# Decoder layer on one core: residual loads moved into the second phase of the down projection, output stores on two queues, three activation splits moved to the end of its first phase

## The chip, the cores and the metric

The kernel runs on one core of one Trainium2 chip. The metric is the device time of one execution in microseconds (us), the median of several runs. A core has five engines that run side by side, each with its own instruction queue worked in order: TensorE (PE, matrix products into the PSUM banks), VectorE (DVE), ScalarE (ACT), GpSimd (POOL) and SyncE (SP), which here only issues transfers (DMAs). ACT can issue DMAs too. Engines wait for each other through semaphores.

## The reference

One decoder layer on 512 positions of 1024 channels in float32: a mixer (a gated matrix memory beside a convolution group), then a convolutional feed-forward block. The change lies in the last lines of the feed-forward block:

```python
def rms_norm(x, g):
    xf = x.astype(jnp.float32)
    y = xf * lax.rsqrt(jnp.mean(xf * xf, axis=-1, keepdims=True) + EPS)
    return (y * g.astype(jnp.float32)).astype(x.dtype)
...
        u = rms_norm(x, ffn_pre_g[l]) * (1.0 + sc2) + sh2
        up = causal_dwconv(u @ ffn_up[l], ffn_conv_w[l], ffn_conv_b[l])
        a, gt = jnp.split(up, 2, axis=-1)
        f = (jax.nn.silu(gt) * a) @ ffn_down[l]
        x = x + g2 * rms_norm(f, ffn_post_g[l])
```

Here `x` on the right is the residual (the mixer's output with its own residual added), `f` the down projection of 2816 channels back to 1024, and `g2` a gate per channel.

## The kernel before

**Number format.** Every large product is made of three matmuls on split operands: a float32 tile is split into a high half (rounded by ACT, `S.activation(hi, src, AF.Copy)`) and a low half (the rest, a subtraction on DVE). `split` (line 925) does it for the down projection; `mm3` (line 186) issues the three matmuls. A matmul of this kind has 128 rows of weights or activations as its stationary operand and 512 columns.

**The down projection** multiplies by a seven-product scheme of Strassen's kind over a 2 x 2 blocking (two halves of the tokens, two halves of the channels on either side). It runs over NM = 11 blocks m of 256 hidden channels, in two phases, since the products and their banks do not fit at once.

- Phase one (the loop at line 1056): `forms1(m)` makes the weight combinations of block m on DVE and splits four of them; `prod1` adds products p1, p5, p7 and p6, two token tiles each (q = 0, 1), 24 matmuls a block. For m = 9 and 10 the products are ordered one by one (line 1067), so that each result can be drained while the next is made. The combination that phase two needs again goes to memory (`t2_d`).
- Phase two (line 1102): `forms_g2(m)` splits the activations of block m, which had been stored to memory by `forms` during the up projection and are read back by `load_g2(m)` into one of five buffers (`kept`): two 256-wide forms side by side (profile names g2h, g2l) and a third (s). `forms2(m)` makes and splits three weight tiles (b, b, t in the profile), loaded by `load2(m)`. `prod2` adds products p2, p3, p4: 18 matmuls a block. For m = 9 and 10 the matmuls stand in the tail, token tile by token tile.
- The tail (line 1113) runs over the four token tiles tt: the last 6 or 12 matmuls, the sum of products (DVE, line 1127), its squares summed on ACT (`sq_sum`, line 610), the factor 1/rms (DVE line 615, POOL line 617), the gate (line 1130), and at line 1134 the factor times the row plus the residual `xr`. The residual stands in memory as `x1_d`, two halves of 512 channels a token tile, written long before. It is loaded on SP at line 1121 into tiles of a pool of four (`cvtile`), and the output rows are stored on SP at line 1135.

**Who sets the order.** On SP and PE the instructions run in the order of the source. On ACT, DVE and POOL a scheduler orders them when the kernel is built, by its own estimate of when operands are there. A tile from a pool waits until the tile that had its buffer before has been read by all its readers: `slot` has 44 buffers, which in phase one hold all split activations (`pairs`, 4 for each of 11 blocks); the weight halves have 20 (`wpool`), and the raw weights four places in all. On SP, the reload `load_g2(m + 5)` needs the buffer of activation m, so it waits for `forms_g2(m)`.

Of the kernel before, what the change touches and what calls it, by code (L numbers as in the profile page):

```python
# [19 lines left out]
T = 512  # L20
KT = D // P
NT = T // P
# [30 lines left out]
def decoder_layer(ctx, tc, w_glu0, x, c, adaT, vecs, w_glu, w_qko, w_v0, w_v, w_out, w_up, w_down, out):  # L53
    nc = tc.nc
# [29 lines left out]
    def slot(name, dt=F32):  # L84
        return slots.tile([P, T], dt, tag="t", name=name)
# [100 lines left out]
    def mm3(ps, a, b, start, stop):  # L186

        PE.matmul(ps, a[0], b[0], start=start, stop=False)  # L188
        PE.matmul(ps, a[0], b[1], start=False, stop=False)  # L189
        PE.matmul(ps, a[1], b[0], start=False, stop=stop)  # L190
# [79 lines left out]
    xr = [slot(f"xr{j}") for j in range(KT)]  # L270
# [10 lines left out]
    def u_tiles(name):  # L281
        hi = upool.tile([P, KT, T], F32R, tag="uh", name=f"{name}h")
        lo = upool.tile([P, KT, T], F32R, tag="ul", name=f"{name}l")
        return hi, lo, [(hi[:, j, :], lo[:, j, :]) for j in range(KT)]

    _, _, u = u_tiles("u")
# [316 lines left out]
    x1_d = [[dram.tile([P, T], F32, tag=f"x1d{tt}_{hf}", name=f"x1d{tt}_{hf}") for hf in range(2)] for tt in range(NT)]  # L603

    def cvtile(name):
        return cvs.tile([P, T], F32, tag="cvs", name=name)

    def sq_sum(src, col, name):
        junk = small.tile([P, T], BF16, tag="junk", bufs=1, name=f"{name}junk")
        S.activation(junk, src, AF.Square, accum_out=col)  # L610

    def token_factor(sq, name):

        t = small.tile([P, 1], F32, tag="tt", name=f"{name}t")
        V.tensor_scalar(out=t, in0=sq[:, :1], scalar1=sq[:, 1:2], scalar2=D * EPS, op0=ALU.add, op1=ALU.add)  # L615
        r = small.tile([P, 1], F32, tag="tr", name=f"{name}r")
        G.tensor_tensor(out=r, in0=t, in1=mhalf[:, :1], op=ALU.pow)  # L617
        return r

    def tok(tt):  # L620
        return slice(tt * P, (tt + 1) * P)
# [298 lines left out]
    NM = NF // 2  # L920
# [4 lines left out]
    def split(src, hi, lo):  # L925
        S.activation(hi, src, AF.Copy)
        V.tensor_tensor(out=lo, in0=src, in1=hi.bitcast(F32), op=ALU.subtract)
# [51 lines left out]
    M2 = NM - 2  # L979
# [11 lines left out]
    def parts(r, names):  # L991
        out = {}
        for name, b in names:
            hi, lo = wpool.tile([P, T], F32R, tag="w", name=f"{name}h"), wpool.tile([P, T], F32R, tag="w", name=f"{name}l")
            split(r[:, b * T : (b + 1) * T], hi, lo)
            out[name[:2]] = (hi, lo)
        return out

    def quarter(r, b):
        return r[:, b * T : (b + 1) * T]  # L1000
# [3 lines left out]
    def load1(m):  # L1004
        loaded[m] = r = wd_raw(m, 1)
        nc.sync.dma_start(r[:, T:], w_down[m][:, T:])

    def forms1(m):

        r = loaded.pop(m)  # L1010
        t3, b11, b12, b22 = (quarter(r, b) for b in range(4))
        V.tensor_tensor(out=t3, in0=b22, in1=b12, op=ALU.subtract)
        V.tensor_tensor(out=b12, in0=b12, in1=b11, op=ALU.subtract)
        V.tensor_tensor(out=b22, in0=b22, in1=b12, op=ALU.subtract)
        w = parts(r, [(f"b1_{m}", 1), (f"t1_{m}", 2), (f"t3_{m}", 0), (f"t2_{m}", 3)])
        nc.sync.dma_start(t2_d[m], b22)
        return w

    def load2(m):
        loaded[m] = r = wd_raw(m + NM, 2)  # L1020
        nc.sync.dma_start(r[:, :T], w_down[m][:, :T])
        nc.sync.dma_start(r[:, T : 2 * T], w_down[m][:, 3 * T :])
        nc.sync.dma_start(r[:, 2 * T : 3 * T], t2_d[m])

    def forms2(m):

        r = loaded.pop(m)
        V.tensor_tensor(out=quarter(r, 2), in0=quarter(r, 0), in1=quarter(r, 2), op=ALU.subtract)
        return parts(r, [(f"b2_{m}", 0), (f"b4_{m}", 1), (f"t4_{m}", 2)])

    def load_g2(m):
        nc.sync.dma_start(kept[:, m % 5, :], g2_d[m])

    def forms_g2(m):
        r = kept[:, m % 5, :]
        h, l, s = slot(f"g2h{m}", F32R), slot(f"g2l{m}", F32R), slot(f"s4{m}", F32R)
        split(r[:, :T], h, l)
        split(r[:, T:], s[:, :HT], s[:, HT:])
        return [(h[:, :HT], l[:, :HT]), (h[:, HT:], l[:, HT:]), (s[:, :HT], s[:, HT:])]

    def part(form, q):
        return tuple(z[:, q * P : (q + 1) * P] for z in form)
# [4 lines left out]
    def prod1(m, which):  # L1047
        (a11, s3), (s1, s2) = (halves_of(z) for z in pairs[m])
        ps, form, w = {"p1": (p1, a11, "b1"), "p5": (p5, s1, "t1"), "p7": (p7, s3, "t3"), "p6": (p6, s2, "t2")}[which]
        for q in range(2):  # L1050
            mm3(ps[q], part(form, q), w1[m][w], m == 0, m == NM - 1)

    w1, w2, g2 = {}, {}, {}
    for m in range(3):
        load1(m)
    for m in range(NM):
        w1[m] = forms1(m)
        if m + 3 < NM:
            load1(m + 3)
        else:  # L1060
            load2(m + 3 - NM)
        if m < 5:
            load_g2(m)
        if m < M1:
            for which in ("p1", "p5", "p7", "p6"):
                prod1(m, which)
# [26 lines left out]
    def prod2(m, which, q):  # L1093
        a12, a22, s4 = g2[m]
        ps, form, w = {"p2": (p2, a12, "b2"), "p3": (p3, s4, "b4"), "p4": (p4, a22, "t4")}[which]
        mm3(ps[q], part(form, q), w2[m][w], m == 0, m == NM - 1)
# [2 lines left out]
        sq_sum(sp5[q], fsq[:, 2 * (2 + q) + 1 : 2 * (2 + q) + 2], f"c22_{q}")  # L1099
    for q in range(2):  # L1100
        V.tensor_tensor(out=sp5[q], in0=sp5[q], in1=g2r[1], op=ALU.mult)
    for m in range(NM):
        g2[m] = forms_g2(m)
        w2[m] = forms2(m)
        if m + 3 < NM:
            load2(m + 3)
        if m + 5 < NM:
            load_g2(m + 5)
        if m < M2:
            for which in ("p2", "p3", "p4"):  # L1110
                for q in range(2):
                    prod2(m, which, q)
    for tt in range(NT):
        q = tt % 2
        for which in ("p2", "p3") if tt < 2 else ("p4",):
            for m in range(M2, NM):
                prod2(m, which, q)
        res, xr = [], []
        for hf in range(2):
            xr.append(cvtile(f"xr{tt}_{hf}"))  # L1120
            nc.sync.dma_start(xr[hf], x1_d[tt][hf])
        for hf, pair in enumerate(((p2[q], sp1[q]), (p3[q], su[q])) if tt < 2 else ((p4[q], s3[q]), None)):
            if pair is None:
                res.append(sp5[q])
                continue
            ps, z = pair
            V.tensor_tensor(out=z, in0=ps, in1=z, op=ALU.add)
            sq_sum(z, fsq[:, 2 * tt + hf : 2 * tt + hf + 1], f"dn{tt}_{hf}")
            m = slot(f"fo{tt}_{hf}")
            V.tensor_tensor(out=m, in0=z, in1=g2r[hf], op=ALU.mult)  # L1130
            res.append(m)
        r = token_factor(fsq[:, 2 * tt : 2 * tt + 2], f"ro{tt}")
        for hf in range(2):
            V.scalar_tensor_tensor(out=res[hf], in0=res[hf], scalar=r, in1=xr[hf], op0=ALU.mult, op1=ALU.add)
            nc.sync.dma_start(out[tok(tt), hf * T : (hf + 1) * T], res[hf])


def _layout(i):
# [65 lines left out]
```

## Time and profile before

| | |
|---|---|
| median of 3 runs | 794.95 us (794.9 to 799.16) |
| the profiled execution | 795.99 us, its span 794.3 us |
| busy: PE | 763.7 us (96%) |
| busy: DVE | 591.8 us (75%) |
| busy: ACT | 408.3 us (51%) |
| busy: POOL | 384.0 us (48%) |
| granted PE clock, mean | 0.99 |
| DMA | 124.28 MB, 156 GB/s from and to memory |

The span runs from the first to the last instruction; the execution's own time holds 1.7 us more around it. All times in the views are us from the start of the span. A row of a timeline has start, length, engine, source line, operation, output and inputs by the program's names (buffer numbers and digits left out, so the quarters t1, t2 and t3 of a block all appear as t), then the shape; in square brackets stands the idle time of the engine before it and what ended that. DVE and ACT overlap the end of one instruction with the start of the next, so the cost of one is the distance between starts. Phase one runs from 669 to 729 us, phase two from there to 777, and the span's last 17 us have no matmul.

### The profile page before, as it was taken

The page shows a single profiled execution, that of the slowest core. Times are in us where ns is not written, and L with a number is a line of the kernel's source. Part 1 is how long each engine was busy: PE and PEld are TensorE (multiplying, and loading weights), DVE is VectorE, ACT ScalarE, POOL GpSimd, SP SyncE. Part 2 cuts the span into 40 slices and gives each one's busy share as a digit, 9 for nine tenths or more (in the row PEclk, how much of TensorE's full clock was granted, in tenths as well). Part 3 has the DMA queues.
Part 4 walks back from the last instruction along what each step waited for, and adds up shares of the span by engine and source line. Part 5 has one row for each costly group of instructions (what it writes and reads, how often), then busy time and mean ns, then how long its engine had stood idle before and what let it go on. Part 6 is the DMA issues. An engine that isn't in the chain of part 4 may idle for free.

```text
span 794.3 us, 10575 instructions
## 1 busy us (share of the span) xinstructions
PE 763.7 (96%) x3683; PEld 636.6 (80%) x3683; DVE 591.8 (75%) x938; ACT 408.3 (51%) x766; POOL 384.0 (48%) x313
## 2 busy tenths in 40 slices
PE   7999999899999999999999999999999999998991
PEld 4778898678888888888889988888888888886880
DVE  6659999999997434546868796665665567997964
ACT  6576428658664455471344454444444434556641
POOL 3789749769788434342851475444444420000001
PEclk9999999999999999999999999999999999999996
DMA  8972312313127331425954654333333222973925
GB/s 290 332 294 106 108 54 106 132 33 110 66 72 230 129 133 54 160 106 206 350 186 151 210 191 152 104 101 121 127 126 116 88 101 97 356 254 98 349 72 185
DMA packets 35977, 124.28 MB, mean 156 GB/s; under 512 B 4146, under 2 KB 5586, under 8 KB 29908
## 3 DMA queue, kind: packets, MB, share of 16 engines
q1 hardware_dynamic: 24660, 96.20, 34.8%
q10 hardware_dynamic: 11264, 27.41, 9.7%
q8 instruction: 29, 0.48, 0.2%
q14 instruction: 24, 0.20, 0.1%
HBM read 112.17 MB, written 11.42 MB: 156 GB/s over the span
## 4 chain that ended last, share of the span: by engine, by line
PE 72%; DVE 15%; DMA 6%; ACT 3%; issue 2%; POOL 1%; SPq 0%; DVEq 0%; POOLq 0%; ACTq 0%
PE up L190 10%; PE up L189 10%; PE up L188 10%; DVE cv L661 5%; PE p L190 3%; PE p L188 3%; PE p L189 3%; PE glu L189 3%; PE glu L190 3%; PE glu L188 3%; PE qko L189 2%; PE qko L188 2%; PE qko L190 2%; PE mixa L190 2%; PE mixa L188 2%; PE mixa L189 2%
## 5 line engine op out<-in xcount | busy, mean ns | idle before, releaser
L661 DVE SCALAR_TENSOR_TENSOR cv<-gt,cvw,cv 128x506 f32<-128x506 f32 (+24 forms) x200 | 134.3, 729 | 0.4
L617 POOL TENSOR_TENSOR ro0r<-ro0t,mhalf 128x1 f32<-128x1 f32 x1 | 0.9, 922 | 128.9 <-DVE ro0t L615 128.9
L171 POOL TENSOR_TENSOR wup_1024l<-wup,wup_1024h 128x512 fp32r<-128x512 f32 x20 | 27.7, 1383 | 31.7 <-ACT wup_1024h L170 31.7
L171 POOL TENSOR_TENSOR wup_0l<-wup,wup_0h 128x512 fp32r<-128x512 f32 x20 | 27.8, 1388 | 29.5 <-ACT wup_0h L170 29.5
L657 POOL TENSOR_TENSOR cs<-cs,cs 128x510 f32<-128x510 f32 (+3 forms) x32 | 41.8, 1306 | 0.2
L171 POOL TENSOR_TENSOR wup_1536l<-wup,wup_1536h 128x512 fp32r<-128x512 f32 x20 | 28.4, 1421 | 27.2 <-ACT wup_1536h L170 27.2
L189 PE MATMUL up<-u2l,wup_0h 128*128 128x512 f32 (+1 forms) x100 | 36.5, 365 | 0.2 <-DVE u2l L830 0.2
L188 PE MATMUL up<-u2h,wup_0h 128*128 128x512 f32 (+1 forms) x100 | 36.5, 365 | 0.0
L188 PE MATMUL up<-u2h,wup_1024h 128*128 128x512 f32 (+1 forms) x100 | 36.5, 365 | 0.0
L190 PE MATMUL up<-u2h,wup_512l 128*128 128x512 f32 (+1 forms) x100 | 36.4, 364 | 0.0
L189 PE MATMUL up<-u2l,wup_1536h 128*128 128x512 f32 (+1 forms) x100 | 36.4, 364 | 0.0
L190 PE MATMUL up<-u2h,wup_0l 128*128 128x512 f32 (+1 forms) x100 | 36.4, 364 | 0.0
L190 PE MATMUL up<-u2h,wup_1536l 128*128 128x512 f32 (+1 forms) x100 | 36.4, 364 | 0.0
L188 PE MATMUL up<-u2h,wup_1536h 128*128 128x512 f32 (+1 forms) x100 | 36.4, 364 | 0.0
L188 PE MATMUL up<-u2h,wup_512h 128*128 128x512 f32 (+1 forms) x100 | 36.4, 364 | 0.0
L189 PE MATMUL up<-u2l,wup_512h 128*128 128x512 f32 (+1 forms) x100 | 36.4, 364 | 0.0
L190 PE MATMUL up<-u2h,wup_1024l 128*128 128x512 f32 (+1 forms) x100 | 36.4, 364 | 0.0
L189 PE MATMUL up<-u2l,wup_1024h 128*128 128x512 f32 (+1 forms) x100 | 36.4, 364 | 0.0
L155 DVE SCALAR_TENSOR_TENSOR junk<-ada,cb 128x1024 bf16<-128x1024 f32 x20 | 30.5, 1525 | 7.5 <-DMA ada<-in_adaT 7.2
L171 POOL TENSOR_TENSOR wup_512l<-wup,wup_512h 128x512 fp32r<-128x512 f32 x20 | 27.2, 1360 | 14.6 <-ACT wup_512h L170 14.6
L655 ACT ACTIVATE cs<-gt,cvw 128x511 f32<-128x511 f32 (+4 forms) x40 | 27.2, 711 | 4.4 <-POOL cs L657 3.7
L171 POOL TENSOR_TENSOR wqko_1024l<-wqko,wqko_1024h 128x512 fp32r<-128x512 f32 x12 | 16.6, 1380 | 22.4 <-PE v L189 12.3
(1061 smaller groups left out, 2687.0 us busy)
## 6 DMA issues: line engine op xcount, KB each, us to landing
wup<-in_w_up SPq DMA_DIRECT2D x22, 1024.0 KB, 8.7
wqko<-in_w_qko SPq DMA_DIRECT2D x12, 1024.0 KB, 4.8
ada<-in_adaT ACTq DMA_DIRECT2D x20, 512.0 KB, 5.9
ada<-in_adaT SPq DMA_DIRECT2D x16, 512.0 KB, 6.0
wo<-in_w_out SPq DMA_DIRECT2D x8, 1024.0 KB, 9.3
spare<-in_adaT ACTq DMA_DIRECT2D x12, 512.0 KB, 8.0
wglu<-in_w_glu SPq DMA_DIRECT2D x5, 1024.0 KB, 7.5
wd<-in_w_down SPq DMA_DIRECT2D x6, 768.0 KB
```

Source lines behind the costliest of these rows:

```text
L155: t = V.scalar_tensor_tensor(out=junk, in0=r, scalar=1.0, in1=cb, op0=ALU.mult, op1=ALU.mult, accum_out=mod[:, i : i + 1])
L171: (eng or G).tensor_tensor(out=lo[:, :n], in0=src, in1=hi[:, :n].bitcast(F32), op=ALU.subtract)
L188: PE.matmul(ps, a[0], b[0], start=start, stop=False)
L189: PE.matmul(ps, a[0], b[1], start=False, stop=False)
L190: PE.matmul(ps, a[1], b[0], start=False, stop=stop)
L617: G.tensor_tensor(out=r, in0=t, in1=mhalf[:, :1], op=ALU.pow)
L655: S.activation(t[:, d:], cvx[j][:, : T - d], AF.Copy, scale=w(CK - 1 - d))
L657: G.tensor_tensor(out=side[:, d:], in0=side[:, d:], in1=t[:, d:], op=ALU.add)
L661: last_tap = V.scalar_tensor_tensor(out=cp[:, d:], in0=cvx[j][:, : T - d], scalar=w(CK - 1 - d), in1=cp[:, d:], op0=ALU.mult, op1=ALU.add)
```

## The change

Three edits at the end of the layer; everything before line 1050 is the same.

- The activations of blocks 0, 1 and 2 (`forms_g2`) are split in the last three turns of phase one's loop (m = 8, 9, 10) instead of at the head of phase two.
- The residual rows of the four token tiles are loaded on SP in turns 5 to 8 of phase two's loop, ahead of `load2(m + 3)`, instead of in the tail. Those of token tiles 2 and 3 take buffers of `slot`, since four `cvtile`s hold the first two.
- The store of each token tile's second half is issued by ACT's queue, the first still by SP's.

```diff
+    G2A = 3
     w1, w2, g2 = {}, {}, {}
...
         if m < 5:
             load_g2(m)
+        if m >= NM - G2A:
+            g2[m - NM + G2A] = forms_g2(m - NM + G2A)
         if m < M1:
...
+    xrs = []
     for m in range(NM):
-        g2[m] = forms_g2(m)
+        if m >= G2A:
+            g2[m] = forms_g2(m)
         w2[m] = forms2(m)
+        if M2 - NT <= m < M2:
+            tt = m - M2 + NT
+            xrs.append([cvtile(f"xr{tt}_{hf}") if tt < 2 else slot(f"xr{tt}_{hf}") for hf in range(2)])
+            for hf in range(2):
+                nc.sync.dma_start(xrs[tt][hf], x1_d[tt][hf])
         if m + 3 < NM:
             load2(m + 3)
...
-        res, xr = [], []
-        for hf in range(2):
-            xr.append(cvtile(f"xr{tt}_{hf}"))
-            nc.sync.dma_start(xr[hf], x1_d[tt][hf])
+        res, xr = [], xrs[tt]
...
-            nc.sync.dma_start(out[tok(tt), hf * T : (hf + 1) * T], res[hf])
+            (nc.scalar if hf else nc.sync).dma_start(out[tok(tt), hf * T : (hf + 1) * T], res[hf])
```

The scheduler orders the changed kernel anew. On PE nothing moves. On DVE and ACT the orders are the same up to phase one's block 3; there the splits of activation 0, 1 and 2 now stand among the weight splits of blocks 3 and 4, and the splits of activations 3 to 7 stand a little earlier in phase two than before. On DVE the last operations of token tile 1 come ahead of the last gate of tile 3.

## The prediction

> **What bounds the kernel now.** I read the page first, then the chain of waits over the last 30 us, then the timelines of the engines at the two places where TensorE (PE) stands still.
>
> ```profile
> span 794.3 us, 10575 instructions
> ...
> PE 763.7 (96%) x3683; PEld 636.6 (80%) x3683; DVE 591.8 (75%) x938; ACT 408.3 (51%) x766; POOL 384.0 (48%) x313
> ...
> PE 72%; DVE 15%; DMA 6%; ACT 3%; issue 2%; POOL 1%; SPq 0%; DVEq 0%; POOLq 0%; ACTq 0%
> ```
>
> The page has PE busy for 96% of this span and the chain on PE for 72% of it, so a change can only pay where PE idles or after its last matmul. The chain of waits shows what follows that last matmul (start us, length us, what):
>
> ```profile
> 776.87 3.10 DMA xr<-x1d
> ...
> 781.88 2.86 DMA xr<-x1d
> ...
> 786.67 3.14 DMA xr<-x1d
> ```
>
> Three transfers of some 3 us each stand on the path: the residual tiles xr of token tiles 1, 2 and 3. Each is issued behind the output store of the tile before, on the same in-order queue (SP). VectorE (DVE) waits for them, as its timeline says; in square brackets is the idle time before an instruction and what ended it:
>
> ```profile
> 779.61 0.21 DVE L615 TENSOR_SCALAR ro3t<-fsq 128x1 f32<-128x1 f32 x1
> 780.06 1.41 DVE L1134 SCALAR_TENSOR_TENSOR fo<-fo,ro1r,xr 128x512 f32<-128x512 f32 x2 [0.24 <-DMA xr<-x1d]
> 784.84 0.75 DVE L1134 SCALAR_TENSOR_TENSOR fo<-fo,ro2r,xr 128x512 f32<-128x512 f32 x1 [3.37 <-DMA xr<-x1d]
> 789.90 0.75 DVE L1134 SCALAR_TENSOR_TENSOR fo<-fo,ro3r,xr 128x512 f32<-128x512 f32 x1 [3.65 <-DMA xr<-x1d]
> 790.57 0.75 DVE L1134 SCALAR_TENSOR_TENSOR sp<-sp,ro3r,xr 128x512 f32<-128x512 f32 x1
> ```
>
> DVE ends at 790.57 + 0.75 = 791.32; the 2.98 us up to the end of the span are the last store and the closing waits. The other place is the switch between the two phases of the down projection, on PE's timeline; the last two rows are the first and the last of the 36 matmuls that close phase two:
>
> ```profile
> 728.70 0.39 PE L190 MATMUL p<-t_10h,fl 128*128 128x512 f32 x1
> 730.10 0.50 PE L188 MATMUL p<-b_0h,g2h 128*128 128x512 f32 x1 [1.01 <-ACT g2h L926]
> ...
> 732.40 0.50 PE L190 MATMUL p<-b_0h,g2l 128*128 128x512 f32 x1 [1.57 <-DVE g2l L927]
> 732.73 0.40 PE L188 MATMUL p<-b_0h,g2h 128*128 128x512 f32 x1
> ...
> 768.79 0.39 PE L188 MATMUL p<-b_9h,g2h 128*128 128x512 f32 x1
> ...
> 776.73 0.39 PE L190 MATMUL p<-t_10h,g2l 128*128 128x512 f32 x1
> ```
>
> Unhindered, a matmul starts every (776.73 - 768.79) / 35 = 0.227 us. The first two gaps of phase two are waits for the high and then the low half of its first activations (g2h by ScalarE, ACT; g2l by DVE).
>
> **The switch.** The fourth matmul of phase two starts at 732.73; without the waits it would start at 728.70 + 4 x 0.227 = 729.61. The edit splits activations 0, 1 and 2 in phase one, so 3.1 us are gone here if nothing else is late. Next in line are the weight halves and the banks:
>
> ```profile
> 728.89 0.63 ACT L926 ACTIVATE b_3h<-wdmore 128x512 fp32r<-128x512 f32 x1 [0.72 <-PE p L189]
> 720.59 0.69 DVE L927 TENSOR_TENSOR b_0l<-wdmore,b_0h 128x512 fp32r<-128x512 f32 x1
> 726.86 1.28 DVE L1081 TENSOR_TENSOR su<-p,sp 128x512 f32<-128x512 f32 x2
> ```
>
> The first weight block's second low half is written by 720.59 + 0.69 = 721.3, 7 us before the switch, its first one earlier still. The banks of the third product come free with the second of the two su additions, at 728.14; PE asks for them twelve matmuls after the switch, at 731.6. ACT's weight splits run about three blocks ahead (b_3h at 728.89, wanted by PE at 728.93 + 3 x 18 x 0.227 = 741.2). Nothing late is seen, and I take the whole 3.1. All later matmuls of phase two follow at their pace: per block DVE has five operations and a half one, 5 x 0.60 + 0.34 = 3.34 us by the pitch below, against 18 x 0.227 = 4.09 us of PE.
>
> **What the early splits cost where they go.** A group is one g2l and one s on DVE:
>
> ```profile
> 734.73 0.70 DVE L927 TENSOR_TENSOR g2l<-g2kept,g2h 128x512 fp32r<-128x512 f32 x1
> 735.33 0.43 DVE L927 TENSOR_TENSOR s<-g2kept,s 128x256 fp32r<-128x256 f32 x1
> 735.67 0.70 DVE L1088 TENSOR_TENSOR sp<-sp,s 128x512 f32<-128x512 f32 x1
> ```
>
> From start to start that is 0.60 + 0.34 = 0.94 us, three groups 2.82 us. In the source the splits stand ahead of blocks 8 to 10 of phase one, but the scheduler that orders ACT and DVE puts them much earlier: on DVE group 0 comes right behind b_3l, group 1 behind the second t_3l, group 2 behind b_4l. There DVE has no free time at all, and its lead over PE is short (first the stretch by engine: length, then busy us of PE, weight loads, DVE, ACT, POOL, then clock, DMA share, GB/s; then what DVE delivers and the matmul that wants it):
>
> ```profile
> 680.00:690.00 10.00, 10.00 (x46) 8.29 (x45) 10.00 (x17) 4.77 (x9) 0.00 (x0) 1.00 0.96 344
> 684.68 1.29 DVE L927 TENSOR_TENSOR t_3l<-wdmore,t_3h 128x512 fp32r<-128x512 f32 x2
> 686.99 0.39 PE L189 MATMUL p<-t_3l,fh 128*128 128x512 f32 x1
> 686.49 0.69 DVE L927 TENSOR_TENSOR t_3l<-wdmore,t_3h 128x512 fp32r<-128x512 f32 x1
> 689.71 0.39 PE L189 MATMUL p<-t_3l,fh 128*128 128x512 f32 x1
> 688.89 1.30 DVE L927 TENSOR_TENSOR t_4l<-wd,t_4h 128x512 fp32r<-128x512 f32 x2
> 692.43 0.39 PE L189 MATMUL p<-t_4l,fh 128*128 128x512 f32 x1
> ```
>
> The first t_3l ends at 685.37 and is wanted at 686.99: 1.62 us of lead, of which group 0 takes 0.94. The last t_3l ends at 687.18 for 689.71: 2.53, less two groups 0.65. The first t_4l ends near 688.89 + 0.69 = 689.58 for 692.43: 2.85, less three groups 0.03. From there the lead grows again, since a block costs DVE seven operations, 4.2 us, and PE 24 matmuls, 5.45 us. So the cover is used up to the last tenth. Ends: 0 when the lead just holds, 2.8 when DVE's whole extra time lands on PE. I take 0.2, by the third margin, with some room for semaphores. ACT has room (4.77 of 10 us busy), but it runs in order: each early split waits for its own load, with t_3h and t_4h queued behind, which DVE and then PE need.
>
> ```profile
> 680.62 0.73 SPq L1032 DMA_DIRECT2D g2kept<-g2d  x1
> DMA to landing us min/median/max: 3.1/6.9/8.4
> ```
>
> The third load, issued at 680.62, lands between 680.62 + 6.9 = 687.5 (median) and 689.0 (longest). In the shifted order DVE reaches group 2 at about 690.1, so this wait costs nothing by these rows.
>
> **The residual loads.** Eight loads of 256 KB move from behind the stores to blocks 5 to 8 of phase two on SP, ahead of the weight loads for blocks 8, 9 and 10. SP is free for that:
>
> ```profile
> 718.50 0.43 SPq L1023 DMA_DIRECT2D wdmore<-t2d  x1
> 733.31 0.33 SPq L1032 DMA_DIRECT2D g2kept<-g2d  x1
> 720.00:730.00 10.00, 9.08 (x41) 7.18 (x39) 8.04 (x14) 6.91 (x14) 0.00 (x0) 1.00 0.21 64
> 740.00:750.00 10.00, 10.00 (x46) 8.28 (x45) 9.54 (x18) 6.03 (x13) 0.00 (x0) 1.00 1.04 377
> ```
>
> Today SP stands from 718.50 to 733.31, because the reload of activation 5 needs the buffer of activation 0, which is split only at the switch. Split early, that wait is gone, and the loads that fill the DMA engines at 740 to 750 (377 GB/s) can spread into 720 to 730, where they move 64 GB/s. The eight residual tiles take 2.1 MB / 377 GB/s = 5.6 us of transfer, less than the some 14 us won. The buffers are free: tiles 0 and 1 use conv tiles, unused since the up projection; tiles 2 and 3 use slots whose last readers are products of phase one. I cost the move itself at nothing; if the cover failed, the last weight loads would come up to 5.6 us later.
>
> At the end DVE's waits of 0.24, 3.37 and 3.65 us go: 7.3 us. What DVE still does there is back to back, and the factors of POOL are computed beside it. ACT now issues four of the stores. Its first stands ahead of the squares of tile 2, and waits for the same DVE result that SP waited for, which comes before that tile's sum anyway: nothing.
>
> **The stores, now bunched.**
>
> ```profile
> out<-fo SPq DMA_DIRECT2D x2, 256.0 KB, 2.1
> ```
>
> The last six of 256 KB leave within about 4 us at DVE's pace, where today loads stood between them. At the 377 GB/s above a store needs 0.70 us and six need 4.2 us, so the last waits little: between 0 and one store's 0.7, and I take 0.2, since the pace nearly fits. The Trainium skill, "DMA: Bandwidth & Descriptors", section "Issuing engines are not separate DMA queues", says that DMAs from several engines run on the same 16 DMA engines and that a second issuer saves the sequencer's time alone. By that rule the second queue would not lessen the bunching, and the sum keeps its 0.2; with separate paths it would be 0. The same page's table gives an HBM limit of about 358 GB/s for a core, with which six stores would take an estimated 4.4 us; the row's 377 GB/s is above it, and decides.
>
> **The sum.** 794.3 - 3.1 - 7.3 + 0.2 + 0.2 = 784.3 us of span. The profiled execution took 795.99, 1.7 more than its span, so 786.0 in its terms; the median of the runs, 794.95, is 1.04 below it: 785.0.
>
> **Rivals.** What can be told from no change here is about 1%, 7.95 us, so 787.0 is the border.
> First: DVE's saturated stretch passes the 2.8 us on to PE. For it speaks a margin of 0.03 us that any late semaphore exceeds; against it, that the lead recovers by more than 1 us a block, so a late start is paid once and only by the excess. All of it: 787.6, within 1%. Chance 0.13.
> Second: at the switch another wait takes the place of the removed one, a bank or a weight half, and the 3.1 us stay: 788.1, within 1%. The 7 us and 3 us of room speak against it. 0.05.
> Third, slower: ACT is held in phase one by an early split whose reload has not landed, and DVE and PE stop behind it. PE wants the first t_4l at 692.43, so landing and the two halves after it hurt from about 691 on, and every us after that is one of PE. To eat the 10 us won, the third load must land after 701, 20 us after its issue, against 8.4 for the longest seen; to be 1% slower, after 709, which gives 803 or more. 0.03 with the rest of such holds.
> Fourth: the move of the loads does not do what it says, since SP reaches them late, and a wait of 3 us stays at the last tile: 788, within 1%. 0.02.
>
> **How the numbers follow.** The forecast has 0.77, with a range of its own from 784.3 (both unknown costs at 0, and a few tenths for the changed order of DVE's last operations) to 786.5 (0.7 for the stores and 1.2 for the stall). Taking in most of the first rival, 8 in 10 lie between 783.9 and 787.7. Faster by over 1%: the forecast and a mild form of the first rival, 0.78; within 1%: 0.19; slower: 0.03.
>
> **What would show it.** In the changed profile: PE without a gap at the switch, its last matmul 3 us earlier; no DVE wait on xr; the next-phase reloads from 719 on; the first matmuls on t_3l and t_4l with gaps of a few tenths at most; the last six stores spaced by about 0.7 us. The prediction is wrong if PE's idle time in phase one adds up to over 2 us, if DVE still waits at the end, or if the span closes more than 4 us after DVE's last operation.

## The result, and the profile after

| | before | after |
|---|---|---|
| median, same chip | 794.92 us (794.9 to 799.16, 4 runs) | 785.51 us (783.59 to 786.46, 4 runs) |
| the profiled execution | 795.99 us, span 794.3 us | 785.76 us, span 784.0 us |
| ratio of the runs, after to before | | 0.9867, 95% interval 0.9835 to 0.9899 |

The changed kernel is faster by 1.3% by this ratio (9.4 us between the medians), and its median is half a microsecond from the forecast of 785.0. The page of the profile after, with its span, the engines' shares and the engines' part of the chain that ended last:

```profile
span 784.0 us, 10572 instructions
...
PE 762.9 (97%) x3683; PEld 636.5 (81%) x3683; DVE 591.6 (75%) x938; ACT 408.1 (52%) x766; POOL 383.9 (49%) x313
...
PE 72%; DVE 17%; DMA 4%; ACT 3%; POOL 2%; issue 1%; SPq 0%; DVEq 0%; POOLq 0%; ACTq 0%
```

The busy times are those of before to within 1 us: nothing is computed less or faster, and the 10 us gone were waits. PE's share of the span rises from 96% to 97%; in the chain, DMA falls from 6% to 4%. The three transfers of residual tiles that have left the end, 9.1 us together, are 1.1 of these two points; the rest is elsewhere in the chain.

The two profiles are compared at four places: the first matmul of phase one, its last one, the last matmul of phase two, and the end of DVE's last operation. PE's first matmul of phase one, before and then after:

```profile
669.08 0.39 PE L188 MATMUL p<-b_0h,fh 128*128 128x512 f32 x1
```

```profile
669.36 0.39 PE L188 MATMUL p<-b_0h,fh 128*128 128x512 f32 x1
```

The next rows of PE's timeline of the kernel after are the last matmul of phase one, the first and the fourth of phase two, and the last:

```profile
729.07 0.39 PE L190 MATMUL p<-t_10h,fl 128*128 128x512 f32 x1
729.29 0.39 PE L188 MATMUL p<-b_0h,g2h 128*128 128x512 f32 x1
...
729.97 0.39 PE L188 MATMUL p<-b_0h,g2h 128*128 128x512 f32 x1
...
773.95 0.39 PE L190 MATMUL p<-t_10h,g2l 128*128 128x512 f32 x1
```

No brackets: PE goes through the switch at its usual pitch. And DVE's timeline at the end, where the brackets of before named xr three times:

```profile
767.57 0.69 DVE L1134 TENSOR_TENSOR sp<-p,sp 128x512 f32<-128x512 f32 x1 [3.87 <-PE p L190]
...
776.23 1.40 DVE L1141 SCALAR_TENSOR_TENSOR fo<-fo,ro1r,xr 128x512 f32<-128x512 f32 x2
777.55 0.68 DVE L1137 TENSOR_TENSOR fo<-s,g2r 128x512 f32<-128x512 f32 x1
778.15 0.20 DVE L615 TENSOR_SCALAR ro3t<-fsq 128x1 f32<-128x1 f32 x1
778.27 0.74 DVE L1141 SCALAR_TENSOR_TENSOR fo<-fo,ro2r,xr 128x512 f32<-128x512 f32 x1
...
779.59 0.74 DVE L1141 SCALAR_TENSOR_TENSOR fo<-fo,ro3r,xr 128x512 f32<-128x512 f32 x1
780.26 0.74 DVE L1141 SCALAR_TENSOR_TENSOR sp<-sp,ro3r,xr 128x512 f32<-128x512 f32 x1
```

From 767.57 on DVE waits for nobody. The span by stages, each length being the difference of two starts (DVE's end is its last start plus its length):

| us | before | after | difference |
|---|---|---|---|
| up to the first matmul of phase one | 669.08 | 669.36 | +0.28 |
| to the last matmul of phase one | 59.62 | 59.71 | +0.09 |
| to the last matmul of phase two | 48.03 | 44.88 | -3.15 |
| to DVE's end (791.32; 781.00) | 14.59 | 7.05 | -7.54 |
| to the end of the span | 2.98 | 3.0 | +0.0 |

The third and the fourth line carry the whole gain. The first is code that the change doesn't touch.

### The profile page after: what moved, and what is told of

Same layout as the page of the kernel before. It is cut to its first block, busy times and chain, and to the rows that moved or that the text cites. A ratio compares the mean times of both kernels' runs of the same rounds, so it can differ in the third digit from the quotient of the medians.

```text
span 784.0 us, 10572 instructions
## 1 busy us (share of the span) xinstructions
PE 762.9 (97%) x3683; PEld 636.5 (81%) x3683; DVE 591.6 (75%) x938; ACT 408.1 (52%) x766; POOL 383.9 (49%) x313
## 4 chain that ended last, share of the span: by engine, by line
PE 72%; DVE 17%; DMA 4%; ACT 3%; POOL 2%; issue 1%; SPq 0%; DVEq 0%; POOLq 0%; ACTq 0%
PE up L189 10%; PE up L190 10%; PE up L188 10%; DVE cv L661 8%; PE p L190 4%; PE p L189 4%; PE p L188 4%; PE glu L189 3%; DMA wglu<-in_w_glu 2%; PE glu L190 2%; PE glu L188 2%; PE mixa L190 2%; PE mixa L188 2%; PE mixa L189 2%; PE mixb L190 2%; PE mixb L189 2%
```

## The experiments

The theory was the prediction's own: two independent gains, 3.1 us at the switch and 7.3 us at the end, the first with its cover in phase one nearly used up. The rivals were that SP is not free for the residual loads unless the early splits go with them, that the second store queue has a part in the gain, and that the early splits cost PE more than a few tenths. Four kernels ran together on one chip (the diffs are against the changed kernel), where the kernel before had a median of 797.39 us (796.0 to 800.76, 7 runs).

### Residual loads alone

```diff
-    G2A = 3
+    G2A = 0
...
-            (nc.scalar if hf else nc.sync).dma_start(out[tok(tt), hf * T : (hf + 1) * T], res[hf])
+            nc.sync.dma_start(out[tok(tt), hf * T : (hf + 1) * T], res[hf])
```

> Only the residual loads are moved; the splits stay at the switch and all stores on one queue. Theory (parts add up): the waits at the end go, 7.3 us, and the switch keeps its 3.1, so some 787.6 us beside 794.9. Rival (the early splits are needed to free SP for the loads): SP still stands until 733, the eight loads fall into the full stretch of the DMA engines, the weights of blocks 8 to 10 come late, and PE loses up to 5.6 us: up to 793.

Measured: 788.17 us (787.65 to 792.31), ratio 0.9896, interval 0.9865 to 0.9928; span of the profile 786.7 us. Its list of PE's waits from 660 us on (what waited, for what, us in all, times, longest):

```profile
PE p L190 <- DVE g2l L927: 1.1, 1, 1.1
PE p L188 <- ACT g2h L926: 1.0, 1, 1.0
```

These are the two waits at the switch, and there is no other. SP's queue of the same kernel shows how the loads fare without the early splits, and the stretch by engine (columns as in the prediction) what the DMA engines do:

```profile
733.20 0.33 SPq L1032 DMA_DIRECT2D g2kept<-g2d  x1
...
757.86 1.01 SPq L1114 DMA_DIRECT2D xr<-x1d  x2
```

```profile
750.00:760.00 10.00, 10.00 (x46) 8.29 (x45) 9.42 (x18) 6.62 (x13) 0.00 (x0) 1.00 1.05 384
```

SP stands until 733.20 as before, the two halves of the last residual tile are issued from 757.86 on, and the DMA engines run at 384 GB/s for another 10 us, with PE still at 10.00 of 10 us busy. DVE's end comes 7.05 us behind the last matmul (783.70 against 776.65), as in the changed kernel. So the loads fit beside the weight loads even where SP is held; the rival falls.

### Early splits alone

```diff
-        res, xr = [], xrs[tt]
+        res, xr = [], []
+        for hf in range(2):
+            xr.append(cvtile(f"xr{tt}_{hf}"))
+            nc.sync.dma_start(xr[hf], x1_d[tt][hf])
```

The loads in phase two's loop are left out, and the stores are on SP.

> Only the three splits are moved. Theory: PE has no gap at the switch, the three waits for residual tiles at the end stay, 794.9 - 3.0 = 791.9 us. Rival (the end is set by something other than PE's last matmul): no change, 794.9.

Measured: 791.9 us (791.77 to 793.05), ratio 0.9935, interval 0.9915 to 0.9955; span 791.3 us. PE has no wait behind 660 us. Its chain of waits shows the end that stayed:

```profile
778.81 2.96 DMA xr<-x1d
...
783.69 3.14 DMA xr<-x1d
```

DVE's end is 14.41 us behind the last matmul, against 14.59 before. The span is 3.0 us shorter than that of the kernel before: phase two takes 44.88 us as in the changed kernel, 3.15 less than before, and the other stages differ by under 0.2 each.

By the ratio the gain is 5.2 us (3.6 to 6.8), more than the traces show, so that the median equals the expected 791.9 to the digit is chance: the kernel before is 2.5 us slower on this chip than the 794.9 that the expectation started from. The granted clock points the same way: the four runs with the splits alone all have a mean clock of 0.990, while the seven runs of the kernel before on this chip have 0.986 to 0.989. No trace of those seven runs shows where they lost it, so this stays open.

From phase one's first matmul on the traces are comparable: the clock is 1.00 as long as PE works (in the changed kernel from 668 to 773 us), and the sizes below are taken from there. From that matmul to the end of the span it is 114.5 us with both parts (next experiment), 117.3 with the loads alone and 122.0 with the splits alone. So the splits are worth 2.7 us on top of the loads, and the loads 7.5 on top of the splits. (With the loads alone the switch itself waits 0.4 us less than before.)

### All stores on SP

```diff
-            (nc.scalar if hf else nc.sync).dma_start(out[tok(tt), hf * T : (hf + 1) * T], res[hf])
+            nc.sync.dma_start(out[tok(tt), hf * T : (hf + 1) * T], res[hf])
```

> The changed kernel with all stores on SP's queue. Theory (a second queue saves only the issue, and stores leave at VectorE's pace): the same as the changed kernel within 0.3 us, 785.5. Rival (one queue cannot take six stores in 4 us): the end comes 1 to 2 us later, 786.5 to 787.5.

Measured: 785.96 us (784.85 to 788.16), ratio 0.9861, interval 0.9835 to 0.9886; span 783.4 us. The last stores on SP's queue, and the time of all stores from issue to landing:

```profile
779.79 0.33 SPq L1142 DMA_DIRECT2D out<-fo  x1
780.45 0.33 SPq L1142 DMA_DIRECT2D out<-sp  x1
```

```profile
DMA to landing us min/median/max: 2.0/2.1/2.1
```

DVE's last operation ends at 780.42, the last store is issued at 780.45, and each lands in 2.0 to 2.1 us, the same as before the change. One queue keeps up with DVE, and the bunched stores don't wait for each other. The second queue is worth nothing that shows; the rival falls.

### The early splits made dearer

The low halves of activations 0 to 2 are computed twice, which doubles what the early splits cost DVE.

```diff
         split(r[:, T:], s[:, :HT], s[:, HT:])
+        if m < 3:
+            V.tensor_tensor(out=l, in0=r[:, :T], in1=h.bitcast(F32), op=ALU.subtract)
+            V.tensor_tensor(out=s[:, HT:], in0=r[:, T:], in1=s[:, :HT].bitcast(F32), op=ALU.subtract)
```

> The changed kernel, with the low halves of the three early activations computed a second time (same values), 2.8 us more on VectorE in blocks 3 to 5 of phase one. Theory (the lead of VectorE over PE is used up there): PE stands 1.9 to 2.8 us in phase one, 787.4 to 788.3 us. Rival (there is lead left): below 0.5 us, 785.5 to 786.

Measured: 788.12 us (786.59 to 791.28), ratio 0.9898, interval 0.9867 to 0.9929; span 784.9 us. PE's timeline, at the start of phase one, in block 4 and at the end of the phase:

```profile
667.94 0.39 PE L188 MATMUL p<-b_0h,fh 128*128 128x512 f32 x1
691.22 0.39 PE L188 MATMUL p<-t_4h,fh 128*128 128x512 f32 x1
692.88 0.50 PE L189 MATMUL p<-t_4l,fh 128*128 128x512 f32 x1 [1.27 <-DVE t_4l L927]
...
729.90 0.39 PE L190 MATMUL p<-t_10h,fl 128*128 128x512 f32 x1
```

Phase one takes 729.90 - 667.94 = 61.96 us, 2.25 more than in the changed kernel, and the only wait that the list of waits names, 1.27 us, is for the tile t_4l that the prediction named as the tightest; smaller gaps at the t_3 and t_4 tiles around it make up the rest. Of 3 x 0.94 = 2.82 us added on DVE, 2.25 reach PE. So the lead that hid the first set of splits is used up by it, and there is no cover for a second. (The profiled span is only 0.9 us longer than the changed kernel's because this execution reached phase one 1.42 us earlier; see the last section.)

### Looking for a better end: the changed kernel again, gate products on GpSimd

What bounds the end now is DVE, which works from 767.57 without a pause and ends 7.05 us behind PE. The theory of the next kernels was that every operation taken from it there, or done before the last matmul, brings the end nearer. The changed kernel and two variants of the gate line ran on another chip (kernel before: 798.22 us, 794.45 to 800.15, 9 runs, the shortest at a mean clock of 0.992, the longest at 0.982):

```diff
-            V.tensor_tensor(out=m, in0=z, in1=g2r[hf], op=ALU.mult)
+            (G if (tt, hf) in ((0, 1), (1, 1), (2, 0)) else V).tensor_tensor(out=m, in0=z, in1=g2r[hf], op=ALU.mult)
```

The second variant has only (0, 1) and (1, 1) on GpSimd.

> The changed kernel once more, beside the two below on one chip. By the four parts so far its span is 784.0 or, where the stretch of halved TensorE clock near 154 us is absent, 1.4 to 2 us shorter; ratio to the kernel before 0.987.

> The changed kernel with three of the six gate products of the tail on GpSimd (second halves of token tiles 0 and 1, first half of tile 2). Theory (after the change the end is set by VectorE's chain of 13.4 us behind the first finished product): 3 x 0.63 us leave the chain; the factors of tiles 1 to 3 wait behind GpSimd's products for some of it, so VectorE ends 1.3 to 1.9 us earlier against TensorE's last matmul, 783.6 to 784.2 us beside 785.5. Rival (GpSimd's products, 1.4 us each, hold the factors): no gain or up to 1 us slower.

> The same with two gate products on GpSimd (second halves of token tiles 0 and 1). Theory: 2 x 0.63 us leave VectorE's chain and nothing waits for GpSimd, 1.0 to 1.3 us earlier, 784.2 to 784.5 us. Rival (the chain is bound by the factors, not by VectorE's load): under 0.3 us.

Measured: the changed kernel 785.12 us (784.25 to 785.6), ratio 0.9841 (0.9816 to 0.9867); three gate products moved 787.17 us (785.58 to 788.34), ratio 0.9868 (0.9841 to 0.9895); two moved 785.85 us (785.1 to 786.78), ratio 0.9852 (0.9826 to 0.9879). The changed kernel's span is 783.4 us here, with the slow stretch near 154 us present (clock 0.66 from 154 to 158), so neither of the two expected lengths came out exactly; it reaches phase one 0.5 us earlier than in the first profile. Both variants miss their theory: DVE's end behind the last matmul is 7.06, 7.76 and 7.49 us, later by 0.7 and 0.4 where 1.3 to 1.9 and 1.0 to 1.3 earlier were expected. Of the 2 us between the medians with three products, the traces explain the 0.7. The view of one tile's factor, of the changed kernel and then of the variant with two, gives shortest, median and longest of the two operations that use it, in ns; then POOL's and DVE's timelines of that variant:

```profile
L1141 DVE SCALAR_TENSOR_TENSOR fo<-fo,ro0r,xr x2: 741/742/744, 771.7 to 772.3; 128x512 f32<-128x512 f32 x2
```

```profile
L1141 DVE SCALAR_TENSOR_TENSOR fo<-fo,ro0r,xr x2: 744/1266/1787, 771.2 to 771.9; 128x512 f32<-128x512 f32 x2
```

```profile
768.69 1.30 POOL L1137 TENSOR_TENSOR fo<-su,g2r 128x512 f32<-128x512 f32 x1 [124.39 <-DVE su L1134]
...
771.47 1.67 POOL L1137 TENSOR_TENSOR fo<-su,g2r 128x512 f32<-128x512 f32 x1 [0.38 <-DVE su L1134]
```

```profile
769.28 0.69 DVE L1134 TENSOR_TENSOR sp<-p,sp 128x512 f32<-128x512 f32 x1 [0.67 <-PE p L190]
```

The second of the two, 0.74 us alone, takes 1.79 us while POOL's product runs from 771.47 to 773.14, and POOL's takes 1.67 us instead of the 1.30 of its first one, beside which DVE read a bank. The Trainium skill, "GPSIMD Engine Reference", section "Specifications", says that GpSimd shares its SBUF interfaces with VectorE and that they contend where a DVE instruction has two SBUF inputs; these operations have two, and the trace agrees. The first of the two still overlaps the same product, from 771.47 to its end near 771.98, and keeps its 744 ns; POOL's product is the longer by 0.37 us. That looks like two engines taking turns rather than both running slower, but no run here separates the two.

The sum of the variant with two comes out. The first product moved frees nothing: the third sum of products starts 1.36 us after the second with the gate product between them (changed kernel) and without it, since DVE then waits 0.67 us for PE. The second spares DVE 0.60 us, and the slow operation costs 1.06 (from the start of the pair to DVE's next start it is 2.38 us instead of 1.32). The difference of 0.46 is the 0.43 by which DVE ends later. So the rival of that kernel, a chain bound by the factors, is not what held it. In the variant with three products the factors, which run on POOL too, queue behind them as its rival said, and DVE waits:

```profile
775.17 1.26 POOL L1137 TENSOR_TENSOR fo<-s,g2r 128x512 f32<-128x512 f32 x1 [1.23 <-DVE s L1134]
776.40 0.99 POOL L617 TENSOR_TENSOR ro1r<-ro1t,mhalf 128x1 f32<-128x1 f32 x1
```

```profile
777.42 1.41 DVE L1141 SCALAR_TENSOR_TENSOR fo<-fo,ro1r,xr 128x512 f32<-128x512 f32 x2 [0.31 <-POOL ro1r L617]
```

### Looking for a better end: three blocks token tile by token tile

With M2 = NM - 3 the last three blocks of phase two, not two, are ordered by token tile, so the results of tiles 0 and 1 come sooner. The second kernel also holds the last two operations of tile 2 behind the factor sum of tile 3 on DVE (the lines that do this are left out here).

```diff
-    M2 = NM - 2
+    M2 = NM - 3
```

> The changed kernel with the last three blocks of phase two, in place of two, ordered token tile by token tile (54 matmuls in the tail in place of 36; the residual loads stand one block earlier). Theory (behind TensorE's last matmul only what VectorE could not do earlier is left): the first product is ready 45 matmuls before the last in place of 30, so VectorE starts its chain 3.4 us earlier, and it ends 1.5 to 2.6 us closer to the last matmul than the 7.05 us of the changed kernel; TensorE itself loses nothing: 783.0 to 784.0 us, ratio 0.981 to 0.983. Rival (the weight halves of block 10, wanted 4 us earlier, are late): TensorE stands up to 3 us in the tail and nothing is won.

> The same, with the factor of token tile 3 ahead of the two last operations of tile 2 on VectorE, so that GpSimd's power runs beside them. Theory: VectorE ends a further 0.5 to 0.9 us closer to TensorE's last matmul, some 5 us behind it. Rival (VectorE's load alone sets the end): no further gain.

Measured, on a third chip (kernel before: 797.68 us, 794.98 to 800.76, 11 runs): 784.93 us (783.47 to 788.17, 6 runs), ratio 0.985 (0.9828 to 0.9871), and 784.28 us (782.44 to 789.12, 6 runs), ratio 0.9842 (0.9817 to 0.9868). DVE ends 6.38 and 5.96 us behind the last matmul. DVE's timeline of the first:

```profile
762.63 0.69 DVE L1134 TENSOR_TENSOR sp<-p,sp 128x512 f32<-128x512 f32 x1 [1.74 <-PE p L190]
...
764.67 0.69 DVE L1134 TENSOR_TENSOR su<-p,su 128x512 f32<-128x512 f32 x1 [0.62 <-PE p L190]
...
776.50 0.20 DVE L615 TENSOR_SCALAR ro3t<-fsq 128x1 f32<-128x1 f32 x1
777.36 0.75 DVE L1141 SCALAR_TENSOR_TENSOR fo<-fo,ro3r,xr 128x512 f32<-128x512 f32 x1 [0.66 <-POOL ro3r L617]
```

The work begins 762.63 us into the span, 9.8 us ahead of the last matmul (772.40) instead of 6.4, but DVE then waits for PE between the products, and at the very end 0.66 us for the last factor, because the scheduler had used up tile 2's operations, which could have stood in that gap. The second kernel puts them there and wins 0.42 us more, a little under the expected 0.5 to 0.9. The first misses its theory: it wins 0.7 us of the 1.5 to 2.6 expected. Its rival is not the reason, since PE has no wait and phase two takes 44.88 us as in the changed kernel. What the theory left out is that DVE's early start is of no use while the next product isn't ready. Both ratios lie in the interval of the changed kernel run again (0.9816 to 0.9867): the traces show a tail shorter by 0.7 and 1.1 us, the times can't tell these kernels from the changed one. None of the four variants beats it by a margin that its runs show.

## Why the prediction held, step by step

**The switch: 3.1 predicted, 3.15 measured.** Phase two takes 44.88 us instead of 48.03 from the last matmul of phase one, and no bank or weight half came late in place of the wait. That was the second rival; it fell with the rows at 729. On top of the residual loads alone, though, the splits are worth 2.7 us, since the waits at the switch are shorter in that kernel.

**The early splits: 0.2 predicted, 0.09 measured, 0 to 0.36 over all traces.** DVE's timeline after, at the three groups, and PE's at the first t_4l:

```profile
683.71 0.68 DVE L927 TENSOR_TENSOR g2l<-g2kept,g2h 128x512 fp32r<-128x512 f32 x1
...
688.60 0.68 DVE L927 TENSOR_TENSOR t_3l<-wdmore,t_3h 128x512 fp32r<-128x512 f32 x1
...
691.61 0.42 DVE L927 TENSOR_TENSOR s<-g2kept,s 128x256 fp32r<-128x256 f32 x1
691.94 0.68 DVE L927 TENSOR_TENSOR t_4l<-wd,t_4h 128x512 fp32r<-128x512 f32 x1
```

```profile
689.99 0.39 PE L189 MATMUL p<-t_3l,fh 128*128 128x512 f32 x1
...
692.71 0.47 PE L189 MATMUL p<-t_4l,fh 128*128 128x512 f32 x1
```

The last t_3l ends at 688.60 + 0.68 = 689.28 and is wanted at 689.99: 0.71 us of lead, where the prediction worked out 0.65. The first t_4l ends at 692.62 and is used at 692.71: 0.09 us were left where the prediction worked out 0.03. The matmul there takes 0.47 us instead of 0.39, and the 0.09 us by which phase one is longer stand there. Phase one takes 59.62 us before the change and 59.61 with the residual loads alone. In the eight traces with the early splits as in the changed kernel it takes 59.61 (twice), 59.62, 59.69, 59.71, 59.74, 59.78 and, in the last kernel with three blocks, 59.97. So the stall is between nothing and 0.36 us, and where there is one it stands at the first t_4l: the margin holds in some executions and is just exceeded in others. That the cover was really at its end, and not simply ample, the doubled splits showed: 2.25 of 2.82 us more went to PE. So the first rival's mechanism is real, in the mild form for which the prediction took its 0.2; that the 0.2 lies inside what the traces show is right reasoning, that the first trace came out at half of it is luck.

**ACT held by an early split (the slower rival).** ACT's timeline after:

```profile
688.25 0.63 ACT L926 ACTIVATE g2h<-g2kept 128x512 fp32r<-128x512 f32 x1 [1.72 <-DMA g2kept<-g2d]
...
689.09 1.14 ACT L926 ACTIVATE t_4h<-wd 128x512 fp32r<-128x512 f32 x2
```

The wait is there, 1.72 us for the third reload, with t_4h queued behind it, as the prediction said; the load landed at 688.2, inside the predicted 687.5 to 689.0 and well before the 691 from which it would have hurt. The step that carried this (landing time plus two halves against 691) was right.

**The residual loads: nothing predicted for the move, nothing measured.** SP's queue after, and two stretches by engine, the same as the prediction showed of before:

```profile
720.38 0.66 SPq L1032 DMA_DIRECT2D g2kept<-g2d  x1
...
753.36 1.37 SPq L1114 DMA_DIRECT2D xr<-x1d  x2
```

```profile
720.00:730.00 10.00, 10.00 (x46) 8.29 (x45) 7.26 (x13) 6.93 (x13) 0.00 (x0) 1.00 0.89 303
740.00:750.00 10.00, 10.00 (x46) 8.29 (x45) 10.00 (x20) 6.11 (x13) 0.00 (x0) 1.00 0.89 282
```

The first reload that stood at 733.31 goes out at 720.38, and the traffic spreads as predicted: 303 GB/s at 720 to 730 (64 before), 282 at 740 to 750 (377 before). The last residual tile is issued at 753.36, 20 us ahead of the last matmul, so the fourth rival had no ground. But the run with the loads alone shows that this argument wasn't needed: with SP held until 733 they still came in time. It was true, and carried nothing.

**The end: 7.3 predicted, 7.5 measured.** The three waits are gone. It was the order of the queue that made them, not the pool of four `cvtile`s: before, the last reader of tile 0's buffers ended at 776.44 and that of tile 1's at 781.47, while the loads of tiles 2 and 3 went out at 781.88 and 786.67, each behind the stores of the tile ahead.

The 0.2 us beyond are overlap. Where nothing is waited for, an operation of DVE starts some 0.08 us before the end of the one ahead (778.15 + 0.20 = 778.35, and the next starts at 778.27). Behind a wait it doesn't: before, 779.61 + 0.21 + 0.24 = 780.06 to the digit. So a wait costs its length and the lost overlap. From the start of tile 3's factor sum to DVE's last start it was 790.57 - 779.61 = 10.96 us before; the same operations take 780.26 - 778.15 = 2.11 after, and the two for tile 1, which now stand ahead, 777.55 - 776.23 = 1.32. The difference is 7.53 us: 7.26 of waits and three times 0.09. That is the whole gain at the end, so the changed order of DVE's last operations, for which the prediction kept a few tenths in its range, was worth nothing.

**The stores: 0.2 predicted, nothing measured.** From DVE's end to the span's end it is 3.0 us with two queues, 3.0 with one, and 2.98 before. The bound of one store's 0.7 us for bunching took no part of the time. The prediction worked out 0.70 us a store from the 377 GB/s of a stretch of loads; the last stores left every 0.66 us, an estimated 397 GB/s, and none landed later than 2.1 us after its issue. So that stretch's rate was not a limit for them.

The four terms erred to the same side, by 0.05, 0.1, 0.2 and 0.2 us, and 0.28 us in code that the change doesn't touch took half of that back: 784.0 us of span for 784.3. The median is off the other way, 785.51 for 785.0, by the last step: the prediction took the median 1.04 us below the profiled execution, as it was before, and it was 0.25 below. The runs of the changed kernel differ by 2.9 us among themselves, so a forecast this close is in part chance; that the terms came out one by one is not.

## What to carry to other kernels

Loads whose data is long in memory belong ahead of the stores on an in-order queue: 7.3 us of waits came from nothing but loads standing behind stores that waited for the tile before. When work is moved into a stretch where its engine is saturated, don't ask for idle time but for the lead of that engine over its reader at each deadline: here it covered 2.8 us to within 0.4, and not a second such load. Moving elementwise work to an idle engine helps only if it doesn't slow the busy one beside it, and if that engine's own small results don't queue behind it.

## What the runs showed besides

**One cold clock window comes and goes.** The stretch of the trace in which PE's clock falls, in the changed kernel and then in the one with doubled low halves (the clock is the third number from the end), and under each the same two matmuls of PE's timeline, one at the start of the stretch and one behind it:

```profile
154.00:158.00 4.00, 3.83 (x11) 3.12 (x12) 3.97 (x10) 1.80 (x3) 1.23 (x1) 0.63 0.39 131
```

```profile
154.16 0.77 PE L533 MATMUL Mb<-Ms,rowsel 128*128 128x512 f32 x1 [2.38 <-DVE Ms L563]
...
158.53 0.39 PE L188 MATMUL qko<-uh,wqko_1536h 128*128 128x512 f32 x1
```

```profile
154.00:158.00 4.00, 4.00 (x19) 3.32 (x18) 3.97 (x9) 2.31 (x3) 1.73 (x2) 1.00 0.37 129
```

```profile
153.66 0.47 PE L533 MATMUL Mb<-Ms,rowsel 128*128 128x512 f32 x1 [2.39 <-DVE Ms L563]
...
156.71 0.39 PE L188 MATMUL qko<-uh,wqko_1536h 128*128 128x512 f32 x1
```

Both kernels are the same up to there. The same work takes 158.53 - 154.16 = 4.37 us in the one and 3.05 in the other, so the slow clock costs 1.3 us; the clock of 0.63 over 4 us gives an estimate of (1 - 0.63) x 4 = 1.5. The Trainium skill, "TensorE: Matmul & The Clock Gate", Part 1, says that PE runs at half clock after an idle window of about 3.4 us, and that the windows run free of the kernel's start, so that the same kernel meets them differently from run to run; 1.3 to 1.5 us lost at half clock is an estimated 3 us of such a window, and in its length the trace agrees. PE's own wait ahead of the stretch is only 2.38 us, behind eight matmuls of four columns, and it is as long (2.39) in the trace that keeps its full clock; no run here shows what decides between the two. Nor is the window all that moves phase one's start, which is at 669.36 in the one trace and at 667.94 in the other: the first kernel with three blocks has the slow stretch too (0.65), and starts phase one at 667.91. Such differences are as large as those that the last experiments looked for, and a comparison by stages is free of them.

**A busy GpSimd more than doubled a VectorE operation**, 744 to 1787 ns, and the loss came to the engine that the move was meant to relieve.
